# Feed-forward up projection on one Trainium2 core: the order of the block products, forms and sums in the two value-unit groups

## The chip, the core and the metric

The kernel runs on one core of one Trainium2 chip. The metric is device time in microseconds (us), the median of several executions of the same program; lower is better. Before the change three executions took 1221.87, 1222.58 and 1226.74 us, so the median is 1222.58 us. The profile is of a further execution, in which every instruction of the five engines was recorded.

## What is computed

Two layers of a decoder trunk over 512 tokens of width 1024, in float32. Each layer has a mixer, a gated feed-forward network (FFN) and a per-layer embedding. The change lies in the FFN alone:

```python
def _conv_ffn(h, w_up, conv_w, conv_b, w_down):
    u = _causal_depthwise_conv(h @ w_up, conv_w) + conv_b
    gate, up = jnp.split(u, 2, axis=-1)
    return (jax.nn.gelu(gate, approximate=False) * up) @ w_down
```

`w_up` is 1024 x 5632, its left half for the gate and its right half for the values; `h` is the normed input, 512 x 1024.

## The kernel before

**Precision.** Each float32 operand is cut into a rounded high part (ScalarE, ACT: `wh`) and the rest, its low part (VectorE, DVE: `wl`), and each product is three matmuls: high by high, high by low and low by high. `cut_blocks` (L854) and `cut_into` (L865) do this to a form of weights, on lines L870 (ACT) and L873 (DVE); `cut` (L134) does it to a plain column, on L151 and L153.

**Seven products in place of eight.** `seven` (L928) multiplies a 1024 x 256 piece of the gate's weights by all tokens in seven block products, as Strassen's scheme in Winograd's variant does it. The tokens stand as forms e1, o1, o2 and s1 to s4, made once per FFN (`operand`, L820); the weights stand as forms `plain`, `t13`, `t2` and `last`. A block product (`block_product`, L916) is 12 matmuls, lines L924 to L926, with 256 columns each, into one half of a PSUM bank. The results gather in three banks W, X and Y: e1 goes to W's left half, which ACT copies to the left halves of X and Y (L940, L941); s1 goes to W's right half, called V, which ACT copies out as `more` (L947); o1 adds to X's left half and s2 to Y's left half; ACT copies Y's left half to X's right half (L950); s3 adds there; ACT copies X's right half to Y's right half (L954); s4 adds to Y's left half and o2 to X's right half. `seven` is a generator, and each `yield` lets its caller put other products between its own.

**Groups.** Each FFN runs 11 groups d = 0 to 10 (L1210), one for each 256 columns of the gate. Besides the gate's seven products a group needs two columns of values, one of 128 with the index 2d and one with 2d + 1. Mostly each is a plain column of 48 matmuls (`value`, L1008, lines L177 to L179), of which 36 stand ahead of the next group's e1 and 12 behind it. In groups 1 and 4 (`pairs_by_blocks`) the columns 2d + 1 and 2(d + 1) are done together as a *unit*: seven block products of the same scheme (`Unit`, L1064), with copies L1077 (e1's), L1083 (`more`), L1086 (Y's left half to X's right half) and L1092 (X's right half to Y's right half). Its o2 (`fourth`) stands behind e1 of group d + 1.

**Sums.** The form t13 is a pair of sums of blocks of weights. For the gate in groups 1 to 3 and for the units these sums are made by DMA (`sum_ahead`, L1023): one plain load of 512 KB (L1029) and two accumulating transfers of 256 KB issued by GpSimd (POOL, L1031), into a tile of the pool `four`. For the gate in the other groups DVE makes them. The value sums of group d are issued in `prepare(d)`, the plain load on ACT's queue.

**Order.** TensorE (PE) executes in the order of the program text (`manual_schedule`). On the other engines a planner orders the instructions when the program is built: of those that its own estimate of times holds ready it takes the one that stands first in the program, and `high_priority(offset=...)` counts an instruction as so many places earlier. `issue_after(x)` puts a block's instructions behind x on x's engine. At run time each engine executes its own list in that order, and an instruction that waits holds up all behind it.

**Buffers.** Raw weights have two tiles (`raw`, loaded through SyncE's queue, SP, lines L1002 and L1112). The cut forms `wh`, `wl` share a ring of three tiles; t2 has tiles of its own, and the unit's t13 a tile of the pool `four`, which has seven. PSUM has four banks called `ps` and four called `pa`. The ring of three makes one form wait for another: in a unit group the gate's plain and t13 take two tiles, the unit's plain form the third, the gate's `last` the tile of gate plain once o1 is done, and the unit's `last` that of gate t13 once s3 is done. So a gate's raw tile is let go, and the next gate's load (L1112) issued, when `last` has been cut.

**The order of products in a unit group** is, on PE: gate e1; the last 12 matmuls of a column; gate s1, o1, s2; unit e1; gate s3; unit s1, o1, s2; gate s4, o2; unit s3, s4; e1 of the next group; unit o2. Value columns are scaled and convolved by `taps` (L976; DVE L979 to L991, ACT L989), and `close` (L1249) applies Gelu and multiplies.

Of the kernel before, what the change touches and what calls it, by code (L numbers as in the profile page):

```python
# [19 lines left out]
P = 128  # L20
# [43 lines left out]
class Kernel:  # L64
# [863 lines left out]
    def seven(self, od, ws, x, keep=None, sooner=0):  # L928
# [12 lines left out]
        nc.scalar.copy(Y[:, left], W[:, left])  # L941
        yield
# [5 lines left out]
        product(X[:, left], plain, 1, x["o1"])  # L948
        product(Y[:, left], t2, 0, x["s2"])
        yield nc.scalar.copy(X[:, right], Y[:, left])  # L950
        with self.tc.high_priority(offset=sooner) if sooner else nullcontext():
            last = self.cut_blocks(od)
        product(X[:, right], t13, 1, x["s3"])
        yield nc.scalar.copy(Y[:, right], X[:, right])  # L954
        product(Y[:, left], last, 1, x["s4"])
        product(X[:, right], last, 0, x["o2"])
        yield X, Y, more

    def ffn(self, i, project, next_gain):
# [8 lines left out]
        with tc.tile_pool(name=f"ffn{i}", bufs=1) as fp:  # L968
# [66 lines left out]
            def sum_forms(raw, both13, behind=None):  # L1035
                ev, od = self.by_parity(raw)
                if behind:
                    b11, b21, b22 = ev[:, :, :P], od[:, :, :P], od[:, :, P:]
                    plain = self.cut_blocks(raw[:, :, :P])
                    four = self.four(fp)  # L1040
                    h, l = (four[:, 2 * u : 2 * u + 2].rearrange("p a b -> p (a b)") for u in range(2))
                    with tc.issue_after(behind.ins):
                        t13 = self.cut_into(h, l, both13)
                    nc.vector.tensor_tensor(b11, b22, both13[:, :, :P], ALU.add)
                    with tc.high_priority(offset=40):
                        t2 = self.cut_blocks(b11, False)
                    nc.vector.tensor_tensor(b21, b21, b11, ALU.add)
                    return plain, t13, t2
# [15 lines left out]
            class Unit:  # L1064


                def __init__(u, raw, ws):
                    u.od = self.by_parity(raw)[1]
                    u.plain, u.t13, u.t2 = ws
                    u.more = places[id(value_sums)][1].rearrange("p j n -> p (j n)")[:, : S // 2]  # L1070

                def first(u):
# [5 lines left out]
                    u.V = W[:, right]  # L1078

                def second(u):  # L1080
# [3 lines left out]
                    self.block_product(u.X[:, left], u.plain, 1, operands["o1"])  # L1084
                    self.block_product(u.Y[:, left], u.t2, 0, operands["s2"])
                    nc.scalar.copy(u.X[:, right], u.Y[:, left])  # L1086
                    u.last = self.cut_blocks(u.od)
# [12 lines left out]
            def prepare(d, behind=None):  # L1100
# [7 lines left out]
                if d in pairs_by_blocks:  # L1108
                    with tc.issue_after(behind.ins):
                        sum_ahead(value_sums, d, DFF + 256 * d + P, nc.scalar)  # L1110
# [1306 lines left out]
```

## Time and profile before

| what | us |
|---|---|
| median of three executions | 1222.58 |
| profiled execution | 1226.54 |
| its span, first to last instruction of the program | 1224.8 |
| PE busy in it | 1194.5 |
| DVE busy | 1002.1 |
| ACT busy | 700.9 |
| POOL busy | 77.0 |

The mean granted TensorE clock was 0.994 of full speed. The two up projections stand, by the first matmul of group 0's e1, from 182.73 us and from 813.33 us of the span on.

In a row of the timeline the columns are start (us), duration (us), engine, line, operation, output and inputs, shapes, count, and in brackets the idle time of the engine before it with what ended it. `PE pa L924` is a matmul on line 924 into a bank called `pa`; buffer numbers are left out. PE's durations overlap, since matmuls are pipelined: in steady state a 256-column matmul starts every 0.113 us and lasts 0.28. In a row of the stretches stand start and end, length, the busy time of each engine with its count of instructions, the granted clock, the busy share of the DMA engines and GB/s. A waits row has the waiting instruction, what released it, the sum, the count and the longest.

### The profile page before, as it was taken

The numbers are of one execution on the slowest core, as the hardware profiler recorded it, in microseconds if no ns is written. First come the engines' busy times: TensorE is split into PE (matmuls) and PEld (weight loads), VectorE is DVE, ScalarE is ACT, GpSimd is POOL, SyncE is SP. The second block draws the span as 40 slices with busy tenths as digits, with TensorE's granted clock in tenths as the row PEclk, the third lists the DMA queues.
The fourth block names the chain that finished last, engine by engine and source line by source line (L and its number), as shares of the span: only waits on it lengthen the run. The fifth ranks groups of instructions, "written<-read, shape, count | busy, mean of one in ns | idle before, by whom it ended". The sixth has DMA issues, their size and how long they took to land.

```text
span 1224.8 us, 20264 instructions
## 1 busy us (share of the span) xinstructions
PE 1194.5 (98%) x8170; PEld 1082.2 (88%) x8170; DVE 1002.1 (82%) x1603; ACT 700.9 (57%) x1166; POOL 77.0 (6%) x90
## 2 busy tenths in 40 slices
PE   9999999899999999999999999998999999999998
PEld 8887789899899989989988988898989999889887
DVE  6786686798999996798879875777989999988595
ACT  7466455555556753666673654555555556645374
POOL 2600201000000000000100002001000000000000
PEclk9999999899999999999999999999999999999999
DMA  7222534352333333222412216236243241432501
GB/s 218 81 94 69 128 99 120 91 168 71 104 104 104 117 126 110 95 76 88 145 59 68 92 48 146 78 105 148 93 114 129 70 138 63 147 110 95 202 5 69
DMA packets 126610, 128.26 MB, mean 105 GB/s; under 512 B 3336, under 2 KB 120770, under 8 KB 126516
## 3 DMA queue, kind: packets, MB, share of 16 engines
q1 hardware_dynamic: 112144, 115.88, 29.2%
q0 software_dynamic: 11984, 8.81, 4.5%
q10 hardware_dynamic: 2388, 2.27, 0.6%
q8 instruction: 64, 1.05, 0.3%
q14 instruction: 30, 0.25, 0.1%
HBM read 124.86 MB, written 2.10 MB: 104 GB/s over the span
## 4 chain that ended last, share of the span: by engine, by line
PE 55%; DVE 17%; DMA 5%; ACT 4%; issue 2%; POOL 0%; ACTq 0%; POOLq 0%; DVEq 0%; SPq 0%
PE ps L177 5%; PE ps L178 5%; PE ps L179 5%; DVE zt L991 4%; PE ps L193 4%; PE ps L191 4%; DVE wl L873 4%; PE ps L200 3%; PE ps L924 3%; DMA four<-in_ffn_w_up_dram 3%; PE ps L926 3%; PE ps L925 3%; PE pa L179 3%; PE pa L177 3%; PE pa L178 3%
## 5 line engine op out<-in xcount | busy, mean ns | idle before, releaser
L153 DVE TENSOR_TENSOR wl<-raw,wh 128x1024 fp32r<-128x1024 f32 (+3 forms) x130 | 149.2, 1150 | 37.8 <-ACT wh L151 35.7
L151 ACT ACTIVATE wh<-raw 128x1024 fp32r<-128x1024 f32 (+4 forms) x134 | 132.5, 992 | 71.0 <-PE ps L178 28.7
L870 ACT ACTIVATE wh<-raw 128x1024 fp32r<-128x1024 f32 x92 | 97.7, 1062 | 118.4 <-DVE raw L1056 42.2
L873 DVE TENSOR_TENSOR wl<-raw,wh 128x1024 fp32r<-128x1024 f32 x92 | 112.6, 1224 | 27.5 <-ACT wh L870 26.6
L991 DVE SCALAR_TENSOR_TENSOR zt<-z,vfa,zt 128x511 f32<-128x511 f32 (+1 forms) x176 | 130.3, 746 | 1.9 <-ACT zt L989 1.5
L989 ACT ACTIVATE zt<-z,vfb 128x512 f32<-128x512 f32 x88 | 70.3, 808 | 23.8 <-DVE z L986 12.8
L179 PE MATMUL pa<-a,wl 128*128 128x256 f32 x288 | 79.6, 276 | 0.0
L178 PE MATMUL pa<-b,wh 128*128 128x256 f32 x288 | 79.6, 276 | 0.0
L177 PE MATMUL pa<-b,wh 128*128 128x256 f32 x288 | 79.6, 276 | 0.0
L179 PE MATMUL pa<-b,wl 128*128 128x256 f32 x288 | 79.6, 276 | 0.0
L177 PE MATMUL pa<-a,wh 128*128 128x256 f32 x288 | 79.6, 276 | 0.0
L178 PE MATMUL pa<-a,wh 128*128 128x256 f32 x288 | 79.6, 276 | 0.0
L191 PE MATMUL ps<-b,wh 128*128 128x512 f32 (+1 forms) x192 | 73.0, 383 | 0.0
L193 PE MATMUL ps<-b,wh 128*128 128x512 f32 (+1 forms) x192 | 72.3, 380 | 0.0
L924 PE MATMUL ps<-four,wh 128*128 128x256 f32 x232 | 64.9, 280 | 1.9 <-ACT ps L950 1.9
L926 PE MATMUL ps<-four,wl 128*128 128x256 f32 x232 | 64.2, 277 | 0.0
L925 PE MATMUL ps<-four,wh 128*128 128x256 f32 x232 | 64.2, 277 | 0.0
L924 PE MATMUL pa<-four,wh 128*128 128x256 f32 x132 | 39.6, 300 | 20.0 <-ACT ps L941 14.0
L177 PEld LDWEIGHTS pa<-b,wh 128*128 128x128 f32 x288 | 54.1, 188 | 0.0
L178 PEld LDWEIGHTS pa<-b,wh 128*128 128x128 f32 x288 | 54.1, 188 | 0.0
L178 PEld LDWEIGHTS pa<-a,wh 128*128 128x128 f32 x288 | 54.1, 188 | 0.0
L177 PEld LDWEIGHTS pa<-a,wh 128*128 128x128 f32 x288 | 54.1, 188 | 0.0
(564 smaller groups left out, 3963.3 us busy)
## 6 DMA issues: line engine op xcount, KB each, us to landing
raw<-in_ffn_w_up_dram SPq DMA_DIRECT2D x42, 1024.0 KB, 5.3
raw<-in_ffn_w_down_dram SPq DMA_DIRECT2D x13, 1024.0 KB, 5.3
raw<-in_hy_w_in_dram SPq DMA_DIRECT2D x8, 1024.0 KB, 5.2
raw<-in_gla_w_in_dram SPq DMA_DIRECT2D x8, 1024.0 KB, 5.1
raw<-in_ffn_w_down_dram SPq DMA_DIRECT2D x8, 768.0 KB, 4.8
raw<-in_ple_w_gate_dram SPq DMA_DIRECT2D x6, 1024.0 KB, 5.1
four<-in_ffn_w_up_dram POOLq DMA_DIRECT2D x20, 256.0 KB, 6.4
raw<-in_hy_w_out_dram SPq DMA_DIRECT2D x16, 256.0 KB, 4.2
```

The costliest lines, as they stand in the source:

```text
L151: nc.scalar.activation(hv, v, AF.Copy)
L153: self.rest_cut = nc.vector.tensor_tensor(lv, v, hv.bitcast(F32), ALU.subtract)
L177: mm(out, lh, rh, start=start, stop=False, **kw)
L178: mm(out, lh, rl, start=False, stop=False, **kw)
L179: mm(out, ll, rh, start=False, stop=stop, **kw)
L191: mm(out, lh, rh, start=first, stop=False, **kw)
L193: end = mm(out, lt, rt, start=False, stop=False, **kw)
L873: nc.vector.tensor_tensor(l, src, h.bitcast(F32), ALU.subtract)
L924: mm(out, wh, xh, start=first and j == 0, stop=False, **kw)
L925: mm(out, wh, xl, start=False, stop=False, **kw)
L926: mm(out, wl, xh, start=False, stop=j == ND // 2 - 1, **kw)
L991: nc.vector.scalar_tensor_tensor(out=y[:, tap:], in0=z[:, : S - tap], scalar=w[:, f : f + 1], in1=y[:, tap:], op0=ALU.mult, op1=ALU.add,)
```

## The change

In the unit groups the gate's seven products run nearly in one piece, and then the unit's. On PE the order becomes: gate e1; the last 12 matmuls of a column; gate s1, s2, o1, s3, s4; unit e1; gate o2; unit s1, s2, o1, s3, s4; e1 of the next group; unit o2. The forms follow: the gate's `last` takes the third tile of the ring, and the unit's plain form that of gate plain, once gate o1 is done. The unit's forms are no longer made in `prepare` of the group but in the group's own iteration, its t13 behind the copy of the gate's e1. Its t2 and the gate's `last` lose their raised priority. The value sums of group d + 1 are issued in `prepare(d)`: for group 1 on POOL's queue between the two gate sums, for group 4 on ACT's queue as before.

```diff
@@ -925,7 +925,7 @@
             mm(out, wh, xl, start=False, stop=False, **kw)
             mm(out, wl, xh, start=False, stop=j == ND // 2 - 1, **kw)
 
-    def seven(self, od, ws, x, keep=None, sooner=0):
+    def seven(self, od, ws, x, keep=None, amid=False):
 
 
         nc = self.nc
@@ -938,21 +938,30 @@
         plain, t13, t2 = ws
         product(W[:, left], plain, 0, x["e1"], True)
         nc.scalar.copy(X[:, left], W[:, left])
-        nc.scalar.copy(Y[:, left], W[:, left])
-        yield
+        yield nc.scalar.copy(Y[:, left], W[:, left])
+        if amid:
+            last = self.cut_blocks(od)
+            yield
         product(V, t13, 0, x["s1"])
         more = V
         if keep is not None:
             more = keep()
             nc.scalar.copy(more, V)
-        product(X[:, left], plain, 1, x["o1"])
-        product(Y[:, left], t2, 0, x["s2"])
-        yield nc.scalar.copy(X[:, right], Y[:, left])
-        with self.tc.high_priority(offset=sooner) if sooner else nullcontext():
+        if amid:
+            product(Y[:, left], t2, 0, x["s2"])
+            copied = nc.scalar.copy(X[:, right], Y[:, left])
+            product(X[:, left], plain, 1, x["o1"])
+            yield copied
+        else:
+            product(X[:, left], plain, 1, x["o1"])
+            product(Y[:, left], t2, 0, x["s2"])
+            yield nc.scalar.copy(X[:, right], Y[:, left])
             last = self.cut_blocks(od)
         product(X[:, right], t13, 1, x["s3"])
         yield nc.scalar.copy(Y[:, right], X[:, right])
         product(Y[:, left], last, 1, x["s4"])
+        if amid:
+            yield
         product(X[:, right], last, 0, x["o2"])
         yield X, Y, more
 
@@ -1032,20 +1041,8 @@
                         x[:, :, u * P : (u + 1) * P], blocks[u, :, :, c + P : c + 2 * P], accum_op=ALU.add
                     )
 
-            def sum_forms(raw, both13, behind=None):
+            def sum_forms(raw, both13):
                 ev, od = self.by_parity(raw)
-                if behind:
-                    b11, b21, b22 = ev[:, :, :P], od[:, :, :P], od[:, :, P:]
-                    plain = self.cut_blocks(raw[:, :, :P])
-                    four = self.four(fp)
-                    h, l = (four[:, 2 * u : 2 * u + 2].rearrange("p a b -> p (a b)") for u in range(2))
-                    with tc.issue_after(behind.ins):
-                        t13 = self.cut_into(h, l, both13)
-                    nc.vector.tensor_tensor(b11, b22, both13[:, :, :P], ALU.add)
-                    with tc.high_priority(offset=40):
-                        t2 = self.cut_blocks(b11, False)
-                    nc.vector.tensor_tensor(b21, b21, b11, ALU.add)
-                    return plain, t13, t2
                 plain = self.cut_blocks(raw[:, :, :P])
                 given = both13 is not None
                 if not given:
@@ -1064,10 +1061,21 @@
             class Unit:
 
 
-                def __init__(u, raw, ws):
-                    u.od = self.by_parity(raw)[1]
-                    u.plain, u.t13, u.t2 = ws
+                def __init__(u, raw, both13):
+                    u.raw, u.both13 = raw, both13
                     u.more = places[id(value_sums)][1].rearrange("p j n -> p (j n)")[:, : S // 2]
+
+                def forms(u, behind):
+                    ev, u.od = self.by_parity(u.raw)
+                    b11, b21, b22 = ev[:, :, :P], u.od[:, :, :P], u.od[:, :, P:]
+                    u.plain = self.cut_blocks(u.raw[:, :, :P])
+                    four = self.four(fp)
+                    h, l = (four[:, 2 * u : 2 * u + 2].rearrange("p a b -> p (a b)") for u in range(2))
+                    with tc.issue_after(behind.ins):
+                        u.t13 = self.cut_into(h, l, u.both13)
+                    nc.vector.tensor_tensor(b11, b22, u.both13[:, :, :P], ALU.add)
+                    u.t2 = self.cut_blocks(b11, False)
+                    nc.vector.tensor_tensor(b21, b21, b11, ALU.add)
 
                 def first(u):
                     left, right = HALVES
@@ -1076,24 +1084,20 @@
                     for x in (u.X, u.Y):
                         nc.scalar.copy(x[:, left], W[:, left])
                     u.V = W[:, right]
+                    u.last = self.cut_blocks(u.od)
 
                 def second(u):
                     left, right = HALVES
                     self.block_product(u.V, u.t13, 0, operands["s1"])
                     nc.scalar.copy(u.more, u.V)
-                    self.block_product(u.X[:, left], u.plain, 1, operands["o1"])
                     self.block_product(u.Y[:, left], u.t2, 0, operands["s2"])
                     nc.scalar.copy(u.X[:, right], u.Y[:, left])
-                    u.last = self.cut_blocks(u.od)
-
-                def third(u):
-                    left, right = HALVES
+                    self.block_product(u.X[:, left], u.plain, 1, operands["o1"])
                     self.block_product(u.X[:, right], u.t13, 1, operands["s3"])
                     nc.scalar.copy(u.Y[:, right], u.X[:, right])
-
                     self.block_product(u.Y[:, left], u.last, 1, operands["s4"])
 
-                def fourth(u):
+                def third(u):
                     right = HALVES[1]
                     self.block_product(u.X[:, right], u.last, 0, operands["o2"])
 
@@ -1105,32 +1109,36 @@
                 if d - 1 not in pairs_by_blocks:
                     with tc.issue_after(behind.ins) if behind else nullcontext():
                         w0 = column(rv, rv.shape[2] // P - 1)
-                if d in pairs_by_blocks:
-                    with tc.issue_after(behind.ins):
-                        sum_ahead(value_sums, d, DFF + 256 * d + P, nc.scalar)
                 rg = self.raw(ND, 256)
                 nc.sync.dma_start(rg, wu[:, :, 256 * d : 256 * d + 256])
                 ev, od = self.by_parity(rg)
                 ws = sum_forms(rg, gate_sums.get(d))
                 values.append(load_values(d))
                 unit = d in pairs_by_blocks
-                steps = self.seven(od, ws, operands, self.aside, 100 if unit else 0)
-                for e in ahead_of.get(d, ()):
+                steps = self.seven(od, ws, operands, self.aside, unit)
+                ahead = ahead_of.get(d, ())
+                for e in ahead[:1]:
+                    sum_ahead(gate_sums, e, 256 * e)
+                if d + 1 in pairs_by_blocks:
+                    with tc.issue_after(behind.ins) if behind else nullcontext():
+                        sum_ahead(value_sums, d + 1, DFF + 256 * (d + 1) + P, nc.scalar if behind else nc.gpsimd)
+                for e in ahead[1:]:
                     sum_ahead(gate_sums, e, 256 * e)
                 if not unit:
                     return steps, w0, column(values[0], 0)
-                rv = values[0]
-                return steps, w0, Unit(rv, sum_forms(rv, value_sums[d], behind))
+                return steps, w0, Unit(values[0], value_sums[d])
+
+            begun = [None]
 
             def begin(d, steps, w):
 
                 if isinstance(w, Unit):
-                    next(steps)
-                    w.fourth()
+                    begun[0] = next(steps)
+                    w.third()
                     return lambda y: taps(y[:, 0], w.Y, NF + 2 * d, w.more)
                 ps = self.pa()
                 value(w, ps, 0, 6)
-                next(steps)
+                begun[0] = next(steps)
                 value(w, ps, 6, ND)
                 return lambda y: taps(y[:, 0], ps, NF + 2 * d)
 
@@ -1209,14 +1217,17 @@
                 close = lambda: None
                 for d in range(groups):
                     g, y = both(), both()
+                    unit = w1c if isinstance(w1c, Unit) else None
+                    if unit:
+                        next(steps)
+                        unit.forms(begun[0])
                     copied = next(steps)
                     with tc.issue_after(copied.ins):
                         close()
-                    unit = w1c if isinstance(w1c, Unit) else None
                     if unit:
+                        next(steps)
+                        next(steps)
                         unit.first()
-                        copied = next(steps)
-                        unit.second()
                         V1 = unit.X
                     else:
                         V1 = self.pa()
@@ -1233,7 +1244,7 @@
                     if d + 1 < groups:
                         steps, w0c, w1c = prepare(d + 1, copied)
                         if unit:
-                            unit.third()
+                            unit.second()
                             w0c = unit
                         else:
                             cut = self.rest_cut
```

## The prediction

> **What bounds the kernel now.** I read the page first, then the waits of TensorE, then the stretches of the groups that the change touches, then the timelines inside them. The page says that TensorE (PE) is the bound:
>
> ```profile
> span 1224.8 us, 20264 instructions
> PE 1194.5 (98%) x8170; PEld 1082.2 (88%) x8170; DVE 1002.1 (82%) x1603; ACT 700.9 (57%) x1166; POOL 77.0 (6%) x90
> ```
>
> Its products are the same before and after, so only its idle time and its slow stretches can change. In the waits of PE (line, who releases it, us in total, count, longest) three rows carry the idle time:
>
> ```profile
> PE pa L924 <- ACT ps L941: 14.0, 9, 4.0
> PE pa L924 <- ACT pa L1092: 6.0, 4, 3.2
> PE ps L924 <- ACT ps L950: 1.9, 2, 1.1
> ```
>
> L924 opens a block product; L941, L950 and L1092 are copies between PSUM banks on ScalarE (ACT). The change touches groups 1 and 4 of both FFNs ("unit groups"). I cut the trace at the first matmul of each group's e1 (us, PE busy, PEld, DVE, ACT, POOL, granted clock, DMA share, GB/s). The rows are, for the first FFN, groups 1, 2, 3, 4, and for the second, groups 1 and 4:
>
> ```profile
> 204.55:232.08 27.53, 21.61 (x170) 20.91 (x169) 19.52 (x27) 15.17 (x24) 3.36 (x3) 0.93 0.50 121
> 232.08:253.83 21.75, 21.75 (x181) 21.75 (x181) 18.18 (x26) 11.51 (x16) 0.00 (x0) 0.94 0.30 98
> 253.83:274.23 20.40, 20.40 (x182) 20.40 (x181) 18.39 (x27) 11.30 (x16) 2.58 (x2) 1.00 0.51 145
> 274.23:298.14 23.91, 21.48 (x170) 21.05 (x169) 18.96 (x26) 12.53 (x21) 0.00 (x0) 0.93 0.34 98
> 835.08:862.23 27.15, 21.41 (x171) 21.01 (x170) 18.48 (x25) 14.59 (x23) 3.37 (x3) 0.94 0.53 126
> 903.02:926.52 23.50, 20.13 (x170) 19.53 (x169) 19.64 (x27) 12.85 (x22) 0.00 (x0) 1.00 0.34 100
> ```
>
> Group 3 is clean: 180 matmuls of 256 columns by the code in 20.40 us, 0.1133 each, so a block product of 12 takes 1.36. From e1 to the next e1 a unit group has 14 such products, less the unit's o2, which falls behind the next e1, plus a column's last 12 matmuls: 168 matmuls, 19.04 us. The excess is 8.49, 4.87, 8.11 and 4.46 us, together 25.9; group 2 of the first FFN starts slow and adds 1.35. **27.3 us** is all that can be won.
>
> Two chains make most of it, here in group 1:
>
> ```profile
> 207.10 1.06 ACT L870 ACTIVATE four<-four 128x1024 fp32r<-128x1024 f32 x1 [5.28 <-DMA four<-in_ffn_w_up_dram]
> 208.89 0.33 ACT L941 COPY ps<-pa 128x256 f32<-128x256 f32 x1
> 209.27 0.38 PE L924 MATMUL pa<-four,wh 128*128 128x256 f32 x1 [1.83 <-ACT ps L941]
> 217.94 0.37 SPq L1112 DMA_DIRECT2D raw<-in_ffn_w_up_dram  x1
> 226.33 1.06 ACT L870 ACTIVATE wh<-raw 128x1024 fp32r<-128x1024 f32 x1 [1.96 <-DMA raw<-in_ffn_w_up_dram]
> 228.94 0.36 ACT L1092 COPY pa<-pa 128x256 f32<-128x256 f32 x1
> 229.35 0.58 PE L924 MATMUL pa<-four,wh 128*128 128x256 f32 x1 [3.24 <-ACT pa L1092]
> 229.95 0.41 PE L926 MATMUL pa<-four,wl 128*128 128x256 f32 x1
> ```
>
> First: ACT stood 5.28 us for the value sums' DMA, with the two copies that PE's s1 needs queued behind it. Second: the next gate's raw load, issued at 217.94 once the gate's last form had let its buffer go, kept ACT until 226.33, and the copy that the unit's s4 needs came behind three more ACT instructions. The last row shows the price behind the price: matmuls of 0.41 us in place of 0.28, the clock of that stretch being 0.93.
>
> **The change, part by part.** *Value sums a group ahead.* Two sums per FFN, one plain load and two accumulating ones each, are issued one group earlier; no byte is added. For group 1 the plain load leaves ACT's queue for POOL's, between gate sums 1 and 2. Behind it there stand the accumulations of gate sum 2, wanted only in group 2, and the norm's power at 194.35:
>
> ```profile
> 194.35 1.04 POOL L209 TENSOR_TENSOR rtok<-rs,mhalf 128x4 f32<-128x4 f32 x1 [44.73 <-DVE rs L208]
> ```
>
> POOL idles 44.73 us before that, and such a sum's issue took it 3.36 us (the POOL column of group 1, gate sum 3), so this costs nothing. It takes the first chain away: s1's wait on L941, 1.83 us idle here and 4.0 at its longest. If a sum were late again, up to that would come back in its group.
>
> *Gate's seven products in one run, last form first.* The gate's `last` now takes the tile that the column lets go 2.72 us after e1's start, 207.3 in group 1; with 1.06 us on ACT, 1.22 on DVE and a little waiting it is whole near 210.5, where now its buffer is let go at 217.9. So the next raw load (217.94 to 226.33 here, 8.4 us) starts some 7 us earlier and lands before ACT wants it: the second chain goes. Late next are the copies themselves. The order was s1 o1 s2, copy, unit e1, s3, copy, three unit products, s4; now it is s1 s2, copy, o1 s3, copy, s4, and the unit runs likewise. Each copy writes one half of a bank and the next product the other half. What that costs, one place shows with ACT idle:
>
> ```profile
> 296.26 0.36 ACT L1092 COPY pa<-pa 128x256 f32<-128x256 f32 x1 [0.69 <-PE pa L926]
> 296.67 0.38 PE L924 MATMUL pa<-four,wh 128*128 128x256 f32 x1 [0.50 <-ACT pa L1092]
> 296.89 0.28 PE L925 MATMUL pa<-four,wh 128*128 128x256 f32 x1
> ```
>
> Idle 0.50 before it is 0.67 start to start over the usual 0.11 (the last matmul started 0.28 before that idle, 0.78 in all), and its own successor follows 0.22 later, 0.11 too late: **0.78 us** per bare copy. Unit s4 pays that today in all four groups (count 4 of the L1092 row). Gate s4 will: it loses three products of cover. That o1 waits too no row shows, since nowhere does o1 follow a copy into its own bank; the bounds are 0 and 0.78, and I take 0.78, as s4 stands to its copy in the same way. So four bare copies per group: 16 x 0.78 = **12.4 us** of excess that remains, where 3.1 are there now.
>
> The Trainium skill ("PSUM — Partial Sum Buffer", PSUM bank collisions raise a hardware error) speaks against this order: two engines may not be in one bank and quadrant at once, whichever columns they touch, so the guard is by bank. The s4 row agrees. By that rule o1's eight waits are certain and the sum stands; without it the sum would be 6.2 us better.
>
> *How late the copies start.* ACT has one queue. In group 4 of the second FFN the four copies of this kind are, with the PE instruction that follows each finished product 0.16 us before its end (for the last, idle 0.50):
>
> ```profile
> 911.98 0.28 PE L924 MATMUL pa<-b,wh 128*128 128x256 f32 x1
> 914.12 0.38 ACT L950 COPY ps<-ps 128x256 f32<-128x256 f32 x1
> 916.08 0.28 PE L924 MATMUL pa<-four,four 128*128 128x256 f32 x1
> 917.83 0.37 ACT L954 COPY ps<-ps 128x256 f32<-128x256 f32 x1
> 920.24 0.28 PE L924 MATMUL ps<-four,wh 128*128 128x256 f32 x1
> 921.00 0.37 ACT L1086 COPY pa<-pa 128x256 f32<-128x256 f32 x1
> 924.65 0.36 ACT L1092 COPY pa<-pa 128x256 f32<-128x256 f32 x1 [1.31 <-PE pa L926]
> 925.06 0.38 PE L924 MATMUL pa<-four,wh 128*128 128x256 f32 x1 [0.50 <-ACT pa L1092]
> ```
>
> They start 1.98, 1.59, 0.60 and 0.09 us after their product's end, mean 1.07; 0.09 is the best there is. Three of them were covered, now none is. I take 0.25 us per copy: the long ones stood behind forms that had waited themselves, and with the sums in place ACT, busy 13 of some 23 us, is mostly free when a product ends. 16 x 0.25 = 4.0 us; the ends are 0 and 16 x 0.98 = 15.7.
>
> *Unit's plain form behind gate o1.* It takes the tile that gate's `last` took: high half on ACT, low half on VectorE (DVE), free at o1's end. Its rows in three of the groups (ACT starts at o1's end), for the fourth o1's last matmul:
>
> ```profile
> 212.05 0.28 PE L926 MATMUL ps<-a,wl 128*128 128x256 f32 x1
> 216.65 1.23 DVE L873 TENSOR_TENSOR wl<-raw,wh 128x1024 fp32r<-128x1024 f32 x1
> 283.62 1.06 ACT L870 ACTIVATE wh<-raw 128x1024 fp32r<-128x1024 f32 x1 [2.40 <-PE ps L925]
> 286.26 1.22 DVE L873 TENSOR_TENSOR wl<-raw,wh 128x1024 fp32r<-128x1024 f32 x1
> 846.58 1.07 ACT L870 ACTIVATE wh<-raw 128x1024 fp32r<-128x1024 f32 x1 [3.65 <-DVE wl L873]
> 847.68 1.23 DVE L873 TENSOR_TENSOR wl<-raw,wh 128x1024 fp32r<-128x1024 f32 x1
> 910.75 1.07 ACT L870 ACTIVATE wh<-raw 128x1024 fp32r<-128x1024 f32 x1 [0.85 <-PE ps L925]
> 914.93 1.23 DVE L873 TENSOR_TENSOR wl<-raw,wh 128x1024 fp32r<-128x1024 f32 x1
> ```
>
> From o1's end to the low half: 5.55, 3.86, 2.33, 5.41 us. Unit e1's third matmul wants it after s3, a bare copy, s4 and two matmuls, 1.36 + 0.78 + 1.36 + 0.23 = 3.7. At today's lags e1 would wait 1.8, 0.2, 0 and 1.7, in all 3.7; but then the unit's t2 stood ahead on DVE, which now follows. Ends 0 and 3.7; I take half, 1.8. The later forms (b11, t2, b21, last) have two products each in hand. Everything else (the forms' instructions, the DMA counts, POOL) is as before.
>
> **Sum.** 12.4 + 4.0 + 1.8 = 18.2 us of excess in place of 27.3: 9.1 us less. The profiled execution took 1226.5 us (span 1224.8 and 1.7 around it), 4.0 above the median of 1222.58 and within the three runs. 1226.5 - 9.1 = 1217.4 on the profile's scale; on the median's scale 1213.5. As some of the 4.0 may be these very stalls, I say **1214**.
>
> **Rivals.** *The copies stay late (slower).* In one run, every copy's delay reaches PE. At the mean of 1.07 over a best of 0.09, 16 x 0.98 = 15.7 us in place of 4.0, with the plain form at 3.7: 12.4 + 15.7 + 3.7 = 31.8, 4.5 more than now; two or three slow stretches behind waits near 2 us, as after 229.35 (about 2.5 us there and into group 2), make that 10, so 1227 to 1236, about 1231. For it: those rows are the same copies. Against it: their causes move away. It decides against the change once the mean extra delay passes (27.3 - 12.4 - 1.8) / 16 = 0.8 us.
>
> A rule of the Trainium skill bears on those slow stretches ("TensorE: Matmul & The Clock Gate", What's actually happening): the clock falls after an idle window of some 3.4 us. The trace does not keep to it: the idle of 3.24 us at 229.35 is a little under that, and in group 4, whose clock was 0.93, less than 2 us was enough:
>
> ```profile
> 279.05 0.44 PE L924 MATMUL pa<-four,wh 128*128 128x256 f32 x1 [1.93 <-ACT ps L941]
> ```
>
> By that rule the slower rival would lose its slow stretches and end near 1227.
>
> *The DMA waits only move (no change).* The next raw load now runs beside gate sum 3, and 8.4 us is what it took in such company. If ACT still meets it, L1092's idle in both groups 1 stays (3.24 above and, of the row's 6.0 over four less two bare 0.5, 1.76; 4.0 over the bare ones, with a slow stretch of 2.5): 6.5 us kept, 1220. Against it speaks the 7 us earlier issue.
>
> *o1 does not wait.* Then 6.2 us more are won: 1208.
>
> **How the numbers follow.** Chances: forecast 0.50 (its own range 1206 to 1219), slower rival 0.24, DMA rival 0.20, o1 rival 0.06. What measurement tells from no change is about 0.5%, 6.1 us: faster means under 1216.5. Of the forecast 0.44 lies there, with o1's 0.06 that is 0.50; within it lie 0.06, the DMA rival's 0.18 and 0.02 of the slower one, 0.26; slower 0.24. From 1205 to 1233 some 0.15 is left out.
>
> **What would show it.** Right: no PE wait on the value sums' ACT form; in each unit group four PE waits near 0.5 us idle, at o1 and s4 of gate and unit; unit groups of 23 to 24 us, clock near 1.00; the next raw load issued before unit e1. Wrong: idle over 1 us at those products, DVE as releaser of unit e1, or 0.41 us matmuls after a bare copy.

## The result, and the profile after

Over 20 runs each, the kernel before took 1226.74 us (median; 1221.80 to 1229.83) and the changed one 1220.24 (1217.01 to 1227.29): a ratio of 0.9955, with a 95% interval from 0.9941 to 0.9969. The change gains about 6.5 us; 9.1 were forecast. The profiled execution took 1220.20 us, against 1226.54 before. The page after:

```profile
span 1218.4 us, 20259 instructions
PE 1194.5 (98%) x8170; PEld 1081.1 (89%) x8170; DVE 1001.7 (82%) x1603; ACT 703.1 (58%) x1166; POOL 78.1 (6%) x92
```

The span fell by 6.4 us. The waits of PE (releaser, total, count, longest):

```profile
PE ps L924 <- ACT ps L961: 7.5, 4, 2.9
PE ps L924 <- ACT ps L952: 2.4, 4, 0.7
PE pa L924 <- ACT pa L1094: 2.0, 4, 0.5
PE pa L924 <- ACT pa L1097: 2.0, 4, 0.5
PE pa L924 <- ACT ps L941: 1.8, 2, 0.9
```

There are exactly the four kinds of bare copies (those with no product of another bank between the copy and the product that needs it) that the prediction counted, each four times: gate's before o1 (L952) and s4 (L961), unit's before o1 (L1094) and s4 (L1097). L1092 now copies the unit's s1 sum and releases no product. Three kinds wait 0.5 to 0.7 us. The fourth, L961, holds 7.5 us.

Cut at each group's e1 as before (length, then busy time by engine, clock, DMA), these are groups 0, 1, 4, 6 and 7 of the first FFN, and 1 of the second, whose group 4 took 23.30 us as well:

```profile
182.64:206.00 23.36, 21.93 (x190) 21.56 (x189) 16.36 (x25) 14.36 (x23) 1.04 (x1) 1.00 0.27 91
206.00:232.32 26.32, 21.81 (x170) 21.01 (x169) 19.73 (x27) 14.90 (x23) 3.43 (x3) 0.94 0.49 120
273.12:296.42 23.30, 20.82 (x170) 19.77 (x169) 20.79 (x28) 14.05 (x24) 0.00 (x0) 1.00 0.28 91
316.82:338.44 21.62, 21.28 (x182) 20.72 (x181) 20.33 (x28) 11.62 (x17) 0.00 (x0) 1.00 0.29 98
338.44:358.84 20.40, 20.40 (x182) 20.40 (x181) 19.17 (x26) 11.59 (x18) 0.00 (x0) 1.00 0.33 104
830.81:858.62 27.81, 23.25 (x170) 22.45 (x169) 19.73 (x27) 14.93 (x23) 3.42 (x3) 0.88 0.45 115
```

The kernel before, in groups 0, 6 and 7 of its first FFN, which the prediction did not show:

```profile
182.73:204.55 21.82, 21.64 (x190) 21.47 (x189) 14.76 (x21) 12.20 (x19) 3.68 (x3) 1.00 0.51 138
318.63:342.77 24.14, 21.57 (x182) 20.80 (x181) 22.90 (x32) 12.67 (x19) 0.00 (x0) 1.00 0.29 91
342.77:364.15 21.38, 20.68 (x182) 20.49 (x181) 19.40 (x26) 11.87 (x18) 0.00 (x0) 1.00 0.30 99
```

So the 6.4 us are, within 0.1, a sum of three parts. The unit groups, with group 2 behind them, give only 2.7 (the forecast's whole 9.1 lay there). Groups 0 take 2.4 (1.54 here, 0.84 in the second FFN). Groups 6 and 7, which no step spoke of, give 6.2 (3.50 here, 2.70 in the second FFN).

What holds L961 is in ACT's timeline of group 1, and what follows in PE's:

```profile
213.89 1.07 ACT L870 ACTIVATE wh<-raw 128x1024 fp32r<-128x1024 f32 x1 [1.66 <-PE ps L925]
214.97 1.28 ACT L1261 ACT_TABLE_LOAD   x1
216.27 1.06 ACT L1261 ACTIVATE zt<-zt 128x1024 f32<-128x1024 f32 x1
217.23 0.61 ACT L870 ACTIVATE t<-raw 128x512 fp32r<-128x512 f32 x1
217.75 0.36 ACT L961 COPY ps<-ps 128x256 f32<-128x256 f32 x1
```
```profile
218.17 0.58 PE L924 MATMUL ps<-four,wh 128*128 128x256 f32 x1 [2.83 <-ACT ps L961]
218.55 0.41 PE L925 MATMUL ps<-four,wh 128*128 128x256 f32 x1
```

Between the unit's plain form and the copy stand the load of the Gelu table, the Gelu of the group before (L1261) and the high half of the unit's t2. PE waits 2.83 us, and its matmuls then run slow (0.41 us each in place of 0.28), as the clock of 0.94 says. The second FFN's group 1 does the same, with 2.88 us and 0.88.

### The profile page after: what moved, and what is told of

It is laid out like the page before. It is cut to its first block, busy times and chain, and to the rows that moved or that the text cites. A ratio compares the mean times of both kernels' runs of the same rounds, so it can differ in the third digit from the quotient of the medians.

```text
span 1218.4 us, 20259 instructions
## 1 busy us (share of the span) xinstructions
PE 1194.5 (98%) x8170; PEld 1081.1 (89%) x8170; DVE 1001.7 (82%) x1603; ACT 703.1 (58%) x1166; POOL 78.1 (6%) x92
## 4 chain that ended last, share of the span: by engine, by line
PE 79%; DVE 12%; ACT 6%; issue 1%; DMA 1%; POOL 0%; ACTq 0%; DVEq 0%
PE ps L177 8%; PE ps L178 7%; PE ps L179 7%; PE ps L924 5%; PE ps L925 5%; PE ps L926 5%; PE pa L178 4%; PE pa L179 4%; PE pa L177 4%; PE ps L193 4%; PE ps L191 4%; PE ps L200 3%; PE pa L924 3%; PE pa L926 3%; PE pa L925 3%; DVE wl L873 3%
## 5 line engine op out<-in xcount | busy, mean ns | idle before, releaser
L179 PEld LDWEIGHTS pa<-b,wl 128*128 128x128 f32 x288 | 54.1, 188 | 0.0
```

The lines of the kernel that those rows point to most:

```text
L179: mm(out, ll, rh, start=False, stop=stop, **kw)
```

## Experiments

My first theory had two parts: the place of the Gelu in ACT's queue cost the unit groups their gain, and POOL's queue cost groups 0 theirs. The rival to the first was that ACT is simply full there, so that something else would make the copy late.

**Gelu behind s3's copy.** Only the place of the previous group's Gelu and product changes, in unit groups:

```diff
                     copied = next(steps)
-                    with tc.issue_after(copied.ins):
+                    closes = next(steps) if unit else copied
+                    with tc.issue_after(closes.ins):
                         close()
                     if unit:
-                        next(steps)
                         next(steps)
```

> The changed kernel, but in the unit groups the previous group's Gelu and product (with the table load ahead of it) are issued behind the gate's s3 copy instead of the s2 copy. Theory A (the size was missed because the s3 copy stands on ScalarE behind the table load of 1.28 us and the Gelu of 1.05, and the clock falls behind that wait): the four waits on that copy, now 2.83, 2.88, 0.89 and 0.89 us idle, go to 0.5; groups 1 go from 26.3 and 27.8 us to about 23, groups 4 from 23.3 to 22.9; all in all 6 to 9 us less than the changed kernel, 1211 to 1214 beside its 1220. Rival B (ScalarE is simply full in these groups: whatever is put behind makes the next copy late): the wait moves to the unit's s1 or o1, the groups keep 26 to 28 us, time 1218 to 1221.

Measured: 1210.85 us, 0.988 of before (0.9856 to 0.9904), 9.4 less than the changed kernel. ACT in group 1, and groups 1 of both FFNs:

```profile
215.10 0.36 ACT L961 COPY ps<-ps 128x256 f32<-128x256 f32 x1 [0.48 <-PE ps L926]
215.48 1.28 ACT L1261 ACT_TABLE_LOAD   x1
```
```profile
205.68:228.55 22.87, 20.69 (x170) 19.72 (x169) 19.73 (x27) 14.73 (x23) 3.43 (x3) 1.00 0.57 139
826.52:849.38 22.86, 20.67 (x171) 19.70 (x170) 19.74 (x27) 14.74 (x23) 3.42 (x3) 1.00 0.56 139
```

All four waits on L961 are 0.5 now, the clock stays at 1.00, and groups 4 took 22.85 and 22.78 us: the four unit groups lose 3.45, 0.45, 4.95 and 0.52 us, 9.4 together. Nothing took the place of the wait; the rival falls.

**Gate sums first.** In group 0 both gate sums are asked for ahead of the value sum:

```diff
-                for e in ahead[:1]:
+                for e in ahead:
                     sum_ahead(gate_sums, e, 256 * e)
                 if d + 1 in pairs_by_blocks:
...
-                for e in ahead[1:]:
-                    sum_ahead(gate_sums, e, 256 * e)
```

> The changed kernel, but in group 0 both gate sums are issued before the value sum, so that they don't queue on GpSimd behind the value sum's plain load, which waits until 152.9 for a free tile. Theory A (that queue pushed all accumulations from 144-150 to 154-163, beside the loads of group 0's weights, and its operands came about 1.5 us late): gate sums again at 144-150, groups 0 back from 23.36 and 22.59 to about 22 us, 1 to 2.4 us less than the changed kernel, 1218 to 1219. Rival B (the same megabyte beside the same loads, order of no matter): groups 0 stay, 1220.

Measured: 1219.17 us, 0.9944 (0.9924 to 0.9964); groups 0 took 23.23 and 23.49 us. This settled nothing, because the edit didn't do what it was for. POOL, in the kernel before, in the changed one and in this one:

```profile
139.96 1.55 POOL L1029 DMA_DIRECT2D four<-in_ffn_w_up_dram  x2 [4.58 <-DVE b L110]
144.36 5.25 POOL L1031 DMA_DIRECT2D four<-in_ffn_w_up_dram  x4 [2.84 <-DMA four<-in_ffn_w_up_dram]
```
```profile
139.88 0.79 POOL L1038 DMA_DIRECT2D four<-in_ffn_w_up_dram  x1 [4.58 <-DVE b L110]
152.93 1.51 POOL L1038 DMA_DIRECT2D four<-in_ffn_w_up_dram  x2 [12.26 <-DVE four L110]
154.43 2.69 POOL L1040 DMA_DIRECT2D four<-in_ffn_w_up_dram  x2
```
```profile
139.85 1.55 POOL L1038 DMA_DIRECT2D four<-in_ffn_w_up_dram  x2 [4.58 <-DVE b L110]
152.90 0.75 POOL L1038 DMA_DIRECT2D four<-in_ffn_w_up_dram  x1 [11.50 <-DVE four L110]
153.64 7.90 POOL L1040 DMA_DIRECT2D four<-in_ffn_w_up_dram  x6
```

The plain loads of the gate sums go out early again, but the value sum's plain load, which waits for a free tile until 152.90, still stands ahead of every accumulation, since these wait for their own plain loads. The same accumulations were issued from 144.36 before.

**Both edits** (the two diffs above together):

> Both edits (Gelu behind the s3 copy, gate sums ahead of the value sum). If both A theories hold the gains add, 7 to 11 us less than the changed kernel: 1209 to 1213. If ScalarE is simply full and the order of sums does not matter: 1220.

Measured: 1212.12 us, 0.9891 (0.9864 to 0.9918): the Gelu edit's gain and nothing on top, as POOL's order was the same as in the run with gate sums first. Groups 0: 23.36 and 22.02.

**Value sums ahead, alone.** The kernel before with only this:

```diff
-                if d in pairs_by_blocks:
-                    with tc.issue_after(behind.ins):
-                        sum_ahead(value_sums, d, DFF + 256 * d + P, nc.scalar)
...
+                if d + 1 in pairs_by_blocks:
+                    with tc.issue_after(behind.ins) if behind else nullcontext():
+                        sum_ahead(value_sums, d + 1, DFF + 256 * (d + 1) + P, nc.scalar if behind else nc.gpsimd)
```

> The kernel before, with nothing but the value sums a group ahead as in the changed kernel. Theory A (the unforeseen gain in groups 6 and 7 comes from VectorE, which no longer idles in group 4 for a value sum): the waits on the e1 copies in the unit groups go (about 10 us of idle), groups 6 and 7 shorten as in the changed kernel (from 24.1 and 21.4 to 21.6 and 20.4 us, 6 us over both FFNs), groups 0 lengthen by 2.4; the unit's s4 waits on the raw load stay: 1210 to 1215. Rival B (groups 6 and 7 gain from the new order of products, whose last form lets the raw buffer go sooner): groups 6 and 7 stay at 24.1 and 21.4, time 1217 to 1220. Rival C (the new waits only move to the unit's s4): 1224 to 1228.

Measured: 1214.88 us, 0.9917 (0.9891 to 0.9942). Groups 0: 23.00 and 22.40. Unit groups with group 2: 10.2 us less than before, of which group 5 of the first FFN gives 1.3 back (21.78 us). Groups 6 and 7: 21.60 and 20.40 in the first FFN, as theory A said, but 23.64 and 20.40 in the second. The waits on the raw load stayed (L1092: 5.3 us in all, four times, 2.6 at the longest).

So this part alone, with a median 10.4 us below the kernel before, seems worth more than the whole change, though its ten executions lie between 1210.75 and 1223.60 and the two intervals just touch. That looked like proof that the new order loses; the opposite run shows that this was too quick.

**Order alone.** The changed kernel, its value sums issued as before:

```diff
+                if d in pairs_by_blocks:
+                    with tc.issue_after(behind.ins):
+                        sum_ahead(value_sums, d, DFF + 256 * d + P, nc.scalar)
...
-                if d + 1 in pairs_by_blocks:
-                    with tc.issue_after(behind.ins) if behind else nullcontext():
-                        sum_ahead(value_sums, d + 1, DFF + 256 * (d + 1) + P, nc.scalar if behind else nc.gpsimd)
```

> The changed kernel with the value sums issued as before (in the group that uses them, on ScalarE's queue); the new order of products and the new places of the forms stay. Theory A (the sums ahead, not the order, gave the gain in groups 6 and 7, and the order by itself loses): groups 0 back to about 21.8, unit groups longer than the changed kernel's 26.3 and 23.3 by 1 to 3 us each since ScalarE stands for the sum's DMA again, groups 6 and 7 near 24 and 21.4: 1226 to 1234. Rival B (the order gives the gain of groups 6 and 7, because the unit's forms no longer wait): groups 6 and 7 stay at 21.6 and 20.4: 1218 to 1223.

Measured: 1215.56 us, 0.9913 (0.9892 to 0.9934). Theory A was wrong: groups 6 and 7 took 21.61 and 20.39 (second FFN 21.60 and 20.41), so the order shortens them without the sums. Groups 0 were back at 21.82 and 21.72. ACT in group 1 of the first FFN:

```profile
206.00 0.36 ACT L941 COPY ps<-pa 128x256 f32<-128x256 f32 x1
206.62 1.06 ACT L870 ACTIVATE four<-four 128x1024 fp32r<-128x1024 f32 x1 [0.26 <-DMA four<-in_ffn_w_up_dram]
...
213.71 0.36 ACT L961 COPY ps<-ps 128x256 f32<-128x256 f32 x1 [0.46 <-PE ps L926]
214.09 1.28 ACT L1259 ACT_TABLE_LOAD   x1
```

Two things are to be seen. The unit's t13 form, which stood 5.28 us for the sum in the kernel before, now comes behind the e1 copies (L941) and finds the sum all but landed, 0.26 us: with the new order the early sum is not needed. And here the planner happened to put L961 ahead of the table load, so that this group 1 took 23.01 us; in the second FFN it did not, PE waited 2.8 us there as well, and that group took 26.56. So of the 6.6 us by which this run's span is shorter than the changed kernel's, 3.3 in this one group are the planner's accident, and 2.4 are groups 0. The two parts of the change each take the same stall away. Together they gain it once, and pay for groups 0.

**Value sum within group 0's stretch.** Over the Gelu edit, the sum for group 1 leaves the queue of the gate sums:

```diff
+                if behind and d + 1 in pairs_by_blocks:
+                    with tc.issue_after(behind.ins):
+                        sum_ahead(value_sums, d + 1, DFF + 256 * (d + 1) + P, nc.scalar)
...
                 late = begin(0, steps, w0c)
+                with tc.issue_after(begun[0].ins):
+                    sum_ahead(value_sums, 1, DFF + 256 + P)
```

> The Gelu edit, and the value sum for group 1 is issued (on GpSimd) behind the copies of group 0's e1, near 184 us, not with the gate sums; so the gate sums' accumulations have nothing ahead of them. Theory A (in the changed kernel all accumulations of group 0 stood on GpSimd behind the value sum's plain load until 154 to 163 us, beside the loads of group 0's forms; the run with the gate sums first left that queue as it was): accumulations back at 144 to 150 us, groups 0 from 23.36 and 22.55 to 21.8 to 22.2 us, 1 to 2.5 us less than the Gelu edit: 1208.5 to 1210. Rival B (groups 0 are late for another reason, or the sum then comes late for group 1): groups 0 stay, or group 1 grows by 1 us or more: 1211 or above.

Measured: 1208.31 us, 0.9856 (0.9834 to 0.9878). The planner issued that sum at 174.62, not near 184, but the point was met. POOL:

```profile
144.25 5.26 POOL L1040 DMA_DIRECT2D four<-in_ffn_w_up_dram  x4 [2.90 <-DMA four<-in_ffn_w_up_dram]
174.62 0.78 POOL L1038 DMA_DIRECT2D four<-in_ffn_w_up_dram  x1 [25.11 <-DVE four L110]
```

Groups 0 took 21.83 and 21.73 us, all of their 2.4 back. The link is the first gate form of group 0, on ACT in the changed kernel and in this one:

```profile
173.21 1.06 ACT L870 ACTIVATE wh<-raw 128x1024 fp32r<-128x1024 f32 x1 [2.85 <-DMA raw<-in_ffn_w_up_dram]
```
```profile
171.41 1.07 ACT L870 ACTIVATE wh<-raw 128x1024 fp32r<-128x1024 f32 x1 [1.14 <-PE ps L193]
```

The raw load that this form needs was issued at 165.32 and at 165.24. With the accumulations beside it, it kept ACT waiting until 173.21; without them the form waits for PE alone.

**Copies covered.** Over the Gelu edit, the products of the unit groups are put so that every copy has a product of another bank behind it; the gate's order is e1, o1, s2, copy, s1, s3, copy, unit's e1, s4, o2:

```diff
         if amid:
             last = self.cut_blocks(od)
             yield
+            product(X[:, left], plain, 1, x["o1"])
+            product(Y[:, left], t2, 0, x["s2"])
+            copied = nc.scalar.copy(X[:, right], Y[:, left])
         product(V, t13, 0, x["s1"])
...
-            product(Y[:, left], t2, 0, x["s2"])
-            copied = nc.scalar.copy(X[:, right], Y[:, left])
-            product(X[:, left], plain, 1, x["o1"])
             yield copied
...
                     if unit:
-                        next(steps)
                         unit.first()
+                        next(steps)
```

The unit's `second` is reordered in the same way, and its s4 moves into `third`, behind the next gate's e1.

> The Gelu edit, and in the unit groups another order of products, in which a copy always has a product of another bank behind it: o1, s2, copy, s1, s3, copy, unit's e1, s4, o2, and the unit likewise, with the next gate's e1 behind its s3 copy. Nothing else is changed. Theory A (a bare copy costs about 0.6 us for want of a product to cover it, four in each of four groups): the four rows of 2.0 to 2.4 us of waits at L952, L961, L1094 and L1097 of the Gelu edit go, the unit groups shorten from 22.85 to between 20.4 and 21.3 us, 6 to 10 us less than the Gelu edit's 1210.9: 1201 to 1205. Rival B (ScalarE's queue is late for the copies whatever the order, or unit's e1, now a product earlier, waits for its plain form): the idle time moves to s3 or unit e1, 1208 to 1212.

Measured: 1200.93 us, 0.9796 (0.9773 to 0.9818). None of the four rows is left. What waits now is below; of the second row 0.73 and 0.80 us are new waits of the unit's e1 in groups 4 for its plain form (rival B's, but small), and all else is in groups 0 and 6:

```profile
PE pa L924 <- ACT ps L941: 2.9, 3, 1.4
PE pa L926 <- DVE wl L873: 2.5, 5, 0.8
```

**Covered copies and the sum in group 0's stretch:**

> Both edits over the Gelu edit. If both A theories hold the gains add: 1199 to 1203. If only the cover counts: 1201 to 1205. If neither: 1210 to 1212.

Measured: 1198.04 us, 0.9773 (0.9748 to 0.9797), the best version: 28 us less than before and 22 less than the changed kernel. Its group 1 has no idle time on PE at all (here the window runs to the unit's o2, and so holds one product more than those above, since the next gate's e1 now stands ahead of the unit's s4):

```profile
204.27:225.10 20.83, 20.83 (x182) 20.77 (x181) 20.07 (x28) 15.13 (x25) 3.42 (x3) 1.00 0.61 152
```

**The same with the sums issued as before:**

> The run with covered copies and the late Gelu, but with the value sums issued as in the kernel before, in the group that uses them, on ScalarE's queue. Theory A (the sums' early issue is not what took ScalarE's stall of 5.28 us away: the unit's forms, now issued behind the gate's e1 copies, meet the landed sum anyway, as the order-only run's 0.26 us suggests): groups 0 at 21.8 us, unit groups as in the run with covered copies and the sum in group 0, 1197 to 1200. Rival B (o1 now follows the e1 copies at once, and the unit's s1 form stands for the sum again): waits of 1 us or more at the unit's e1 or s1 or at the gate's s3 in some unit groups, 1201 to 1207.

Measured: 1199.03 us, 0.9774 (0.975 to 0.9799), 1.0 us above the last, with executions that overlap (1197.85 to 1202.36, and 1197.31 to 1198.66): in the best order, too, the early sums are worth nothing that the times tell. Rival B's sign is there once: gate's s3 waits 1.09 us for its copy (L947) in group 1 of the second FFN.

**Why groups 6 and 7 gain.** The two single runs left one thing in common with the changed kernel: VectorE no longer stands 3.5 us into group 4 for the unit's t13 form (2.67 us idle in the first FFN before). That idle time would leave it behind. I gave the run with the Gelu edit and the sum in group 0's stretch that much extra work in group 4:

```diff
+                    if d == 4:
+                        with tc.issue_after(copied.ins):
+                            for _ in range(4):
+                                nc.vector.tensor_tensor(R, R, R, ALU.max)
```

> The run with the late Gelu and the value sum in group 0, with four extra operations of 128x512 on VectorE (the maximum of a tile with itself, which changes nothing) issued in group 4 of each FFN, about 2.4 us, as much as VectorE stood idle there in the kernel before (2.67 and 2.26 us). Theory A (the groups 6 and 7 of the kernel before were longer because that idle time left VectorE behind, and it has no slack to catch up until then): groups 6 and 7 grow from 21.6 and 20.4 us towards 24 and 21.4, 1 to 3 us per FFN, with the waits on VectorE's forms and the e1 copies in group 6 back; 1210.5 to 1214.5 beside 1208.3. Rival B (VectorE's idle time of some 2.3 and 2 us in groups 4 and 5 takes it up, and another cause made groups 6 and 7 longer): groups 6 and 7 unchanged, 1208 to 1209.5.

Measured: 1208.21 us, 0.9845 (0.982 to 0.987), groups 6 and 7 unchanged. In that form the theory falls: of VectorE's idle time in groups 4 and 5, a stretch of 1.47 us went and one of 1.96 shrank to 1.40, and the rest of the lag was gone by group 5's last form, which came at 9.70 as without the work. What was left to test was the lag itself, put behind that idle time:

```diff
                     nc.vector.tensor_tensor(z, ps, R, ALU.mult)
+                    for _ in range(4 if f == NF + 9 else 0):
+                        nc.vector.tensor_tensor(z, z, z, ALU.max)
```

> Again the run with the late Gelu and the value sum in group 0, and again four extra 128x512 operations on VectorE per FFN (2.4 us), but now behind its last idle time there: on the tile of the taps that it starts 2.9 us into group 5 (the maximum of the tile with itself). In the kernel before, VectorE reached the low half of the gate's last form 12.3 and 11.5 us into group 5, in the changed kernel at 9.7 in both FFNs; the four operations put ahead in group 4 left it at 9.7, since 2 us of idle time took them up. Theory A (that lag itself makes groups 6 and 7 longer: the raw load that waits for the form, and the forms behind it): the form at about 12, groups 6 from 21.6 to 23.4 to 24.5 us, groups 7 from 20.4 to about 21, 1212 to 1215.5 beside 1208.3. Rival B (the lag is not the cause): the form at about 12, groups 6 and 7 at 21.6 and 20.4, 1208 to 1209.5.

Measured: 1216.25 us, 0.9928 (0.9903 to 0.9952), 7.9 more than without. Groups 5 and 6 of the first FFN, and the low half of group 5's last form on VectorE:

```profile
290.96:312.40 21.44, 20.72 (x183) 20.52 (x181) 19.46 (x29) 12.03 (x18) 0.00 (x0) 1.00 0.27 89
312.40:336.80 24.40, 21.61 (x183) 20.82 (x181) 22.16 (x30) 12.20 (x19) 0.00 (x0) 1.00 0.29 96
```
```profile
304.40 1.22 DVE L873 TENSOR_TENSOR wl<-raw,wh 128x1024 fp32r<-128x1024 f32 x1
```

That form comes 13.44 us into its group, where the kernel before has it at 12.33 and the changed one at 9.71 (groups 5 begin at 298.14 and 296.42):

```profile
310.47 1.22 DVE L873 TENSOR_TENSOR wl<-raw,wh 128x1024 fp32r<-128x1024 f32 x1
```
```profile
306.13 1.22 DVE L873 TENSOR_TENSOR wl<-raw,wh 128x1024 fp32r<-128x1024 f32 x1
```

Group 6 grew by 2.8 us, to the 24.1 of the kernel before and a little beyond, and PE waits for VectorE at its e1, as it did then. Here are the waits with the lag put in, and that e1 in the kernel before:

```profile
PE pa L926 <- DVE wl L873: 3.0, 4, 0.8
```
```profile
319.96 0.38 PE L926 MATMUL pa<-a,wl 128*128 128x256 f32 x1 [0.94 <-DVE wl L873]
```

What lies between is the raw load of group 6, issued 0.06 us behind that form in all three: at 305.68 with the lag put in, 6.72 us ahead of the group, and, before and after the change, 6.88 and 9.41 us ahead:

```profile
311.75 0.37 SPq L1112 DMA_DIRECT2D raw<-in_ffn_w_up_dram  x1
```
```profile
307.41 0.37 SPq L1113 DMA_DIRECT2D raw<-in_ffn_w_up_dram  x1
```

That this load is the link, the second FFN of the run with the value sums alone bears out. VectorE was not late there (the form came at 9.70, the load was issued 9.41 us ahead), but the load kept ACT until 1.62 us before group 6, and the group took 23.64:

```profile
934.34 1.07 ACT L870 ACTIVATE wh<-raw 128x1024 fp32r<-128x1024 f32 x1 [2.22 <-DMA raw<-in_ffn_w_up_dram]
```

So it is shown that VectorE's lag in group 5 makes group 6 long; group 5 paid 1.04 here as well. Group 7 stayed at 20.40, where before had 21.38, so the 1.9 us that groups 7 gained stay unexplained. That the lag of the kernel before came from the sum's wait in group 4 is only argued: 2.4 us of work there was not enough, and the kernel before idled at other places of that group too.

## Why the prediction was right and wrong

- **Bare copies, 16 at 0.78 us: right.** The four rows stand in the trace with 0.50 to 0.7 us of idle time (L961's shortest is 0.89), o1's among them, as the bank rule of the Trainium skill ("PSUM — Partial Sum Buffer", PSUM bank collisions raise a hardware error) had it. Covering them gave 9.9 and 10.3 us, net of some 1.5 us of new waits at the unit's e1 in groups 4; 12.4 were reckoned.
- **How late the copies start: the step that failed.** It put 0.25 us on each copy, 4.0 in all, because ACT would be "mostly free when a product ends". Measured by moving the Gelu: 9.4 us, all at one copy (L961) in each group, 5.5 of it idle time beyond the bare 0.50 and the rest mostly the slow matmuls behind. The unit groups of the changed kernel held 24.6 us of excess where 18.2 were forecast; without the 9.4 they hold 15.2. I started from four copies with a mean delay of 1.07, and reckoned that what had made them late would go with the sums. In truth an instruction that the diff does not touch, the Gelu of the group before with its table load, is issued behind the copy of s2 (`copied`) as before, and this copy now has a bare one close behind it. The slower rival had the mechanism (a copy's delay reaches PE, and slow matmuls follow) but not its place.
- **Unit's plain form late, 1.8 us: nothing.** No wait of the unit's e1 is in the rows, also not with the Gelu moved.
- **Value sums a group ahead "cost nothing": wrong.** They cost 2.4 us in groups 0. The cover that I named, POOL's idle 44.73 us, was the wrong resource: behind the value sum's load stood the accumulations of both gate sums, and these met the raw load of group 0. That the sums took the first chain away was true of the sums alone, but the order does it too.
- **DMA waits only move: no.** In group 1 the next raw load was issued at 212.27 in place of 217.94, and no PE wait on it is left. That the measured time is this rival's 1220 is chance; it came about in another way.
- **Groups 6 and 7: not seen.** They gave 6.2 us. For the 4.3 in groups 6 the path is shown: VectorE less late in group 5, the raw load issued earlier. What made VectorE late before is only argued, and the 1.9 in groups 7 stay open. The prediction looked at what PE waits for inside the unit groups and at no engine's lag behind them.
- **The scale.** The span shortened by 6.4 us where 9.1 were forecast: 6.4 too little in the unit groups and 2.4 lost in groups 0, less 6.2 found in groups 6 and 7. The median of the kernel before over 20 runs is 1226.7, not 1222.6, so the forecast on the profile's scale, 1217.4, was the nearer one.

## What to carry to other kernels

When an order of products is changed, list what else hangs on the points that move: an instruction that is issued behind a copy goes with that copy. Here 2.3 us of such instructions in front of a bare copy cost 9.4 us, more than the 6.5 that the change still gained. Count a copy between banks as free only with a product of another bank behind it; here 16 of them were worth 10 us, and such an order existed. If two edits each remove one stall, measure each alone: here each gained some 10.5 us alone (3.3 of the order's by the planner's accident), and both together 6.5.

## What the runs showed of the hardware

The clock fell after 2.83 and 2.88 us without a matmul, and stayed at 1.00 in the groups whose longest wait was 0.9. The Trainium skill ("TensorE: Matmul & The Clock Gate", What's actually happening) speaks of an idle window of some 3.4 us; these waits are shorter. Nor does the length alone decide: in the run with gate sums first a wait of 2.83 us, up to 843.75, left the clock at 1.00, and in the kernel before one of 1.93 us, up to 279.05, halved it. These are the stretches around the first and behind the second:

```profile
838.00:845.63 7.63, 4.80 (x40) 4.60 (x41) 7.56 (x11) 5.45 (x7) 2.61 (x2) 1.00 0.98 204
```
```profile
279.24:282.65 3.41, 3.41 (x17) 3.41 (x17) 3.41 (x6) 1.58 (x2) 0.00 (x0) 0.50 0.00 0
```

In the kernel before, the clock's records turn to 0.50 at 228.04, 279.24 and 842.44, which lie 15 and 165 times 3.413 us apart, and each time for 3.41 or 6.83 us. That fits a fixed grid of 3.413 us in which a step counts that is mostly idle: 1.93 us of idle fell into the step that ends at 279.24. In the other run the grid, counted from its one fall at 217.58, has a boundary at 842.22, which cuts the wait into 1.30 and 1.53 us.

The table load took 1.28 us, and the Gelu began 0.02 us behind its end (214.97 and 216.27). The Trainium skill ("ScalarE: Activation LUTs", What ACT_TABLE_LOAD costs) gives 1283 ns for the load, which agrees, and some 1380 ns for a drain with it, of which this row shows nothing.

The same raw load, issued 9.41 us ahead of group 6 in both, was waited for in the second FFN of the run with covered copies and not in that with the sum in group 0's stretch besides; group 6 took 23.70 and 21.61 us. ACT in the one (in the other it did not wait for that load):

```profile
920.43 1.06 ACT L870 ACTIVATE wh<-raw 128x1024 fp32r<-128x1024 f32 x1 [2.28 <-DMA raw<-in_ffn_w_up_dram]
```

The same load was late in the second FFN of the run with the value sums alone (2.22 us of waiting) and of the run with covered copies and the sums issued as before (1.72 us; group 6 took 23.10). What made it land late stays open.
